# A state space front re-ordered: powers times coefficient first, its store moved to ScalarE, the first input products behind half a gate block

## The chip, the core and the metric

The kernel runs on one core of a Trainium2 chip. A core has a matrix engine (TensorE, PE in the profile), a vector engine (VectorE, DVE), a scalar engine (ScalarE, ACT), a general engine (GpSimd, POOL) and a synchronisation engine (SyncE, SP) that issues most of the transfers. Each engine runs its own list of instructions in the order in which it is written; semaphores tie the lists together. The metric is device microseconds (us) of one launch, median over several runs.

## The reference, cut to what matters

The network is a two-layer trunk over 1024 frames of 1024 channels. Layer 0 projects the normalised input to 6144 channels, which feed a state space branch (input u, gate), a retention branch (q, k, v, gate) and then one output projection; layer 1 is a convolution module. The change touches only the head of the state space branch. There each of 64 groups has 64 complex states, and from the step and the decay come the powers of the decay and a coefficient that scales the input matrix B:

```python
    lb_re = mag * jnp.cos(aim * dt)          # lambda-bar, one complex number per group and state
    lb_im = mag * jnp.sin(aim * dt)
    nr, ni = lb_re - 1.0, lb_im
    den = are * are + aim * aim
    coef_re = (nr * are + ni * aim) / den
    coef_im = (ni * are - nr * aim) / den
    bb_re = coef_re[..., None] * bre - coef_im[..., None] * bim
    bb_im = coef_re[..., None] * bim + coef_im[..., None] * bre
    ...
        bu_re = jnp.einsum('tbgh,gnh->tbgn', u_c, bb_re)
        bu_im = jnp.einsum('tbgh,gnh->tbgn', u_c, bb_im)
```

The states then run through a scan and are mapped back to channels by C, plus a skip term. All arithmetic is float32.

## The kernel before, in words

Everything is held transposed, channels on the 128 partitions, frames along the free side. A weight block is 128 output channels: it is loaded (`wf_`), split by ScalarE into a rounded high part (`wh_`) and by VectorE or GpSimd into a rest (`wl_`). A product of a block with one half of the frames (512) is 8 pieces of the inner dimension times three matmuls (lines 268 to 270: high times high, high times rest, rest times high), so a half block is 24 matmuls. The blocks come in a fixed sequence: `u0` to `u7` (the state space input), `g8` to `g23` (gates of both branches), then keys, queries, values and the later stages. Three banks of the accumulator (`ps_mm`) are used in turn by the halves, so a half can begin when the half three before it has been read out. A `u` half is read out by VectorE into `ut_` (line 464), a gate half into `gt_` (line 479).

Beside the `u` blocks VectorE works out the state space tables from the parameters (`s5_params`, lines 655 to 853): step, decay, sine and cosine, powers `s5_pr`, `s5_pi` (0 to 8), phases `s5_e1`, `s5_e2`, and the coefficient `s5_cfr`, `s5_cfi` (lines 820 to 839). Then two things use the coefficient: VectorE multiplies eight powers by it, six operations of 128x256 (line 842, helper line 676), giving `s5_pcr` and `s5_pci`; and GpSimd multiplies B by it, four products and two sums of 128x512 (lines 848 to 853), giving `s5_bbr` and `s5_bbi`.

`s5_turned` (line 871) turns `s5_pc` on TensorE (four 128x128 transposes into `turn`), ScalarE copies the bank to `turned` (line 882), and SyncE stores it to `pt_d` (line 883). ScalarE also copies `s5_bbr`, `s5_bbi` into block-diagonal form (`s5_bdr`, `s5_bdi`, line 887, two copies each).

The state space branch works in eight blocks B of 128 channels. For a block, `s5_tables` lets GpSimd make rotation tables `Tc`, `Ts` and the output table `W3` (lines 864 to 866, twelve operations), ScalarE make `R8` (line 939), and `s5_w2` load the turned powers from `pt_d`, spread over 16 partitions each (`PTr`, `PTi`, line 897), and B itself (`BTr`, `BTi`, line 901). ScalarE copies `PTr`, `PTi` to two banks (`pw0`, `pw1`, line 907), and six VectorE operations (lines 909 to 914) give the input matrices `W2r`, `W2i`. `s5_states` multiplies them with the input `U` (loaded by `s5_load`, line 944): eight matmuls of `v0` from `W2r` and eight of `v1` from `W2i` (line 962; the profile records each of these full float32 matmuls as two). The eight `kp` matmuls (lines 971, 973; 16 records) make the local kernel from `W3` and `s5_bd`; VectorE reads them as `Kg` (lines 976, 977), SyncE stores them to `k_d` in eight pieces and loads them back as `Wd` (lines 988, 992), and ScalarE copies that to `W1` (line 1027). VectorE turns and scans the states (lines 998 to 1005) and turns them back to `S` (lines 1012 to 1018). The `y` matmuls (lines 1044, 1048) use `S`, `W3`, `W1` and `U`.

The instructions are put in order by a scheduler that plays the program against a cost model and takes the oldest that is ready in that play; hand-written rules bind it: `ORDER` (lines 41 to 84) names an engine, a late instruction and an early one that has to come first, and `s5_order` (line 87) does so for VectorE in all eight blocks. `issue_after` adds such a rule for all instructions in its body.

Of the kernel before, what the change touches and what calls it, by code (L numbers as in the profile page):

```python
# [15 lines left out]
ALU = mybir.AluOpType  # L16
# [3 lines left out]
P = 128  # L20
# [20 lines left out]
ORDER = (  # L41
    ('PE', ('turn', 0), ('mm_u6_0', 23)),
    ('PE', ('mm_u6_1', 0), ('turn', 3)),
    ('PE', ('mm_g8_0', 0), ('v1_0', 7)),
    ('PE', ('kp_0', 0), ('mm_g8_0', 23)),
    ('PE', ('mm_g8_1', 0), ('kp_0', 7)),
    ('DVE', ('kraw_3', 0), ('yn_2', 0)),
    ('SP', ('gs1_3', 0), ('t_d', 7)),
    ('DVE', ('cv6_0', 23), ('h1l0_1', 0)),
# [89 lines left out]
class Trunk:  # L139
# [515 lines left out]
    def s5_params(self, sp, tp):  # L655
        nc, A = self.nc, self.A
        v = nc.vector
        n_ = [0]
        NP = 32

        def t(shape=(NP,), dt=F32, keep=None):
            n_[0] += 1
            if keep:
                return sp.tile([P, *shape], dt, name=keep)
            return tp.tile([P, *shape], dt, name=f"s5t{n_[0]}", tag=f"s5t_{'x'.join(map(str, shape))}_{dt}",
                           bufs=4 if shape[0] in (3, 4, 8) else 8)
# [8 lines left out]
        def tt(o, a, b, op, eng=v):  # L675
            return eng.tensor_tensor(o, a, b, op=op)
# [54 lines left out]
        r = t((2, NP))  # L731
# [86 lines left out]
        with self.tc.issue_after(self.last_phase.ins):  # L818
# [10 lines left out]
            cfr, cfi = t(keep="s5_cfr"), t(keep="s5_cfi")  # L829
# [10 lines left out]
        self.pc = [tp.tile([P, 8, NP], F32, name=f"s5_pc{c}") for c in "ri"]  # L840
        bc = lambda q: q[:].unsqueeze(1).broadcast_to([P, 8, NP])
        cmul(self.pc[0][:], self.pc[1][:], pr_[:, :8], pi_[:, :8], bc(cfr), bc(cfi), (8, NP))
        self.bb = [sp.tile([P, NP, 16], F32, name=f"s5_bb{c}") for c in "ri"]
        bc = lambda q: q[:].unsqueeze(2).broadcast_to([P, NP, 16])
        x2 = [tp.tile([P, 2, NP, 16], F32, name=f"s5bb{i}", tag="sq", bufs=2) for i in range(2)]
        x1 = [x2[i // 2][:, i % 2] for i in range(4)]
        gp = nc.gpsimd
# [23 lines left out]
    def s5_turned(self, pool):  # L871


        nc = self.nc
        self.pt_d = self.dram.tile([2, 2, P, P], F32, name="pt_d")
        ps = self.bank("turn")
        for c in range(2):
            for a in range(2):
                nc.tensor.transpose(ps[:, (2 * c + a) * P:(2 * c + a + 1) * P],
                                    self.pc[c][:, 4 * a:4 * a + 4, :].rearrange("p a b -> p (a b)"), self.ident[:])  # L880
        t = self.mid.tile([P, 4, P], F32, name="turned")
        nc.scalar.copy(t[:].rearrange("p q n -> p (q n)"), ps[:])
        nc.sync.dma_start(self.pt_d[:].rearrange("c a r n -> r (c a) n"), t[:])
        for q, t in zip(self.bd, self.bb):
            for g in range(2):
                r = slice(64 * g, 64 * g + 64)
                nc.scalar.copy(q[r, :, 16 * g:16 * g + 16], t[r])

    def s5_w2(self, B):

        nc, v = self.nc, self.nc.vector
        (ptr, pti), (btr, bti) = ([self.big(f"{n}{c}_{B}", f"{n}{c}", 1) for c in "ri"] for n in ("PT", "BT"))
        dp, db = self.pt_d, self.A["s5_bt"]

        with self.tc.issue_after(self.u_load.ins) if B else nullcontext():
            for c, pt in enumerate((ptr, pti)):
                nc.sync.dma_start(pt[:].rearrange("p q n -> p (q n)"),
                                  bass.AP(tensor=dp.tensor, offset=dp.offset + (c * 2 * P + 4 * B) * P,
                                          ap=[[32 * P, 8], [0, 16], [1, 4 * P]]))
            for c, bt in enumerate((btr, bti)):  # L900
                nc.sync.dma_start(bt[:].rearrange("p q n -> p (q n)"),
                                  bass.AP(tensor=db.tensor, offset=db.offset + (c * 4 * P + 4 * B) * P,
                                          ap=[[0, 8], [32 * P, 16], [1, 4 * P]]))
        w2r, w2i = (self.big(f"W2{nm}_{B}", f"W2{nm}", 1)[:].rearrange("p q n -> p (q n)") for nm in "ri")
        pr, pi = (self.ps_s5.tile([P, HALF], F32, name=f"pw{c}_{B}", tag=f"y{c}") for c in range(2))
        for bank, t in ((pr, ptr), (pi, pti)):
            nc.scalar.copy(bank[:], t[:].rearrange("p q n -> p (q n)"))  # L907
        br, bi = (t[:].rearrange("p q n -> p (q n)") for t in (btr, bti))
        v.tensor_tensor(w2r, pr[:], br, op=ALU.mult)
        v.tensor_tensor(w2i, pr[:], bi, op=ALU.mult)  # L910
        v.tensor_tensor(pr[:], pi[:], bi, op=ALU.mult)
        v.tensor_tensor(pi[:], pi[:], br, op=ALU.mult)
        v.tensor_tensor(w2r, w2r, pr[:], op=ALU.subtract)
        v.tensor_tensor(w2i, w2i, pi[:], op=ALU.add)
        return [t.rearrange("p (q n) -> p q n", q=4) for t in (w2r, w2i)]
# [25 lines left out]

    def s5_load(self, B):
        U = self.s5.tile([P, 8, P], F32, name=f"U_{B}", tag="U", bufs=2)
        self.u_load = self.nc.sync.dma_start(U[:], self.u_d[B].rearrange("j h g m -> (j h) g m"))
        return U

    def s5_states(self, B):
# [1100 lines left out]
```

## Time and profile before

| | us |
|---|---|
| median of 3 runs | 1133.97 (1131.9 to 1135.23) |
| the profiled execution's own time | 1132.57 |
| its span, first to last instruction | 1130.8 |
| TensorE busy in the span | 1116.0 |
| VectorE, GpSimd, ScalarE busy | 824.5, 592.8, 497.1 |
| mean granted TensorE clock | 0.994 of full speed |

The first column of a timeline row is the start in us from the span's start, the second the time to the end of the row's last instruction; then come engine, line, operation, output and inputs by the program's names without their numbers, and how many instructions the row merges. `[x <-E n Lm]` behind a row is idle time of the engine before it, and what ended it. SPq and ACTq are the sequencers of SyncE and ScalarE issuing a transfer: the row shows the issue, not the transfer. A matmul row's time overlaps that of the next; the pace is read from start to start. PEclk is the granted TensorE clock, 1.00 being full speed.

### The profile page before, as it was taken

What the parts mean: (1) busy time and instruction counts of PE and PEld (TensorE: products, weight loads), DVE (VectorE), ACT (ScalarE), POOL (GpSimd) and SP (SyncE); (2) the same over time, 40 slices, a digit from 0 to 9 for tenths busy, and PEclk for the clock granted to TensorE, in tenths of its full rate; (3) what the DMA queues carried; (4) which work ended last, traced back from release to release, by engine and by line L of the source; (5) the groups of instructions that cost most, each with busy time, mean ns of one, the idle gap of its engine ahead of it and who ended that gap; (6) DMA issues with size and microseconds to landing.
All of it is one profiled execution on the core that took longest, in us unless ns stands there. A gap on an engine that the chain in (4) does not pass through costs nothing.

```text
span 1130.8 us, 17173 instructions
## 1 busy us (share of the span) xinstructions
PE 1116.0 (99%) x6254; PEld 980.1 (87%) x6254; DVE 824.5 (73%) x1481; ACT 497.1 (44%) x729; POOL 592.8 (52%) x410
## 2 busy tenths in 40 slices
PE   9998999999999999999999999999999999999997
PEld 8877888888888888989888888888888888888886
DVE  7895777676516477696668532599999899999744
ACT  7322333333223231324346423545535677446773
POOL 3059766663126344333475110589544568778963
PEclk9998999999999999999999999999999999999999
DMA  8336455555468856958999998665778655356965
GB/s 321 114 104 203 141 170 192 172 183 166 144 234 284 305 185 191 320 192 309 384 387 311 330 332 282 196 230 202 239 257 290 243 193 177 124 173 222 331 256 179
DMA packets 125445, 261.99 MB, mean 232 GB/s; under 512 B 19760, under 2 KB 49328, under 8 KB 124720
## 3 DMA queue, kind: packets, MB, share of 16 engines
q1 hardware_dynamic: 121904, 248.30, 64.8%
q10 hardware_dynamic: 3456, 12.58, 2.8%
q8 instruction: 49, 0.80, 0.3%
q14 instruction: 36, 0.29, 0.1%
HBM read 182.53 MB, written 74.12 MB: 227 GB/s over the span
## 4 chain that ended last, share of the span: by engine, by line
PE 88%; DVE 5%; DMA 3%; ACT 1%; issue 1%; POOL 1%; SPq 0%; POOLq 0%; ACTq 0%; DVEq 0%
PE mm_g L268 7%; PE mm_g L269 7%; PE mm_g L270 7%; PE mm_wo L268 5%; PE mm_wo L270 5%; PE mm_wo L269 5%; PE mm_b L269 2%; PE mm_b L270 2%; PE mm_a L269 2%; PE mm_a L268 2%; PE mm_b L268 2%; PE mm_a L270 2%; PE mm_oc L269 2%; PE mm_oc L270 2%; PE mm_oc L268 2%; PE mm_glu L268 2%
## 5 line engine op out<-in xcount | busy, mean ns | idle before, releaser
L1660 DVE SCALAR_TENSOR_TENSOR cv<-u,convw,cv 128x512 f32<-128x512 f32 x390 | 268.0, 751 | 6.5 <-ACT cv L1627 4.4
L1621 POOL TENSOR_TENSOR tp<-tp,tp 128x512 f32<-128x512 f32 x64 | 82.5, 1289 | 33.4 <-ACT tp L1620 32.5
L268 PE MATMUL mm_g<-xh,wh_g 128*128 128x512 f32 x256 | 98.4, 384 | 0.0
L269 PE MATMUL mm_g<-xl,wh_g 128*128 128x512 f32 x256 | 97.4, 381 | 0.0
L270 PE MATMUL mm_g<-xh,wl_g 128*128 128x512 f32 x256 | 96.1, 380 | 0.0
L530 POOL TENSOR_TENSOR s1q<-s1q,s1q 128x512 f32<-128x512 f32 x12 | 17.2, 1432 | 80.6 <-ACT s1q L525 71.9
L1620 ACT ACTIVATE tp<-u,convw 128x512 f32<-128x512 f32 x64 | 45.3, 718 | 31.6 <-POOL tp L1621 30.9
L479 DVE TENSOR_TENSOR gt<-mm_g,R 128x512 f32<-128x512 f32 x32 | 22.0, 688 | 50.6 <-PE mm_g L270 50.6
L268 PEld LDWEIGHTS mm_g<-xh,wh_g 128*128 128x128 f32 x256 | 48.6, 190 | 7.2 <-ACT pw L907 0.3
L270 PEld LDWEIGHTS mm_g<-xh,wl_g 128*128 128x128 f32 x256 | 48.7, 190 | 7.0
L269 PEld LDWEIGHTS mm_g<-xl,wh_g 128*128 128x128 f32 x256 | 48.7, 190 | 6.7
L269 PE MATMUL mm_oc<-zl,wh_woc 128*128 128x512 f32 (+1 forms) x144 | 51.4, 357 | 0.2 <-DVE zl L1375 0.2
L268 PE MATMUL mm_oc<-zh,wh_woc 128*128 128x512 f32 (+1 forms) x144 | 51.1, 364 | 0.0
L270 PE MATMUL mm_oc<-zh,wl_woc 128*128 128x512 f32 (+1 forms) x144 | 50.8, 356 | 0.0
L268 PE MATMUL mm_wo<-ysh,wh_wos 128*128 128x512 f32 x128 | 48.9, 382 | 0.0
L268 PE MATMUL mm_g<-h1h,wh_cg 128*128 128x512 f32 x128 | 48.9, 382 | 0.0
L269 PE MATMUL mm_u<-xl,wh_u 128*128 128x512 f32 x128 | 48.8, 385 | 0.0
L270 PE MATMUL mm_b<-h1h,wl_cb 128*128 128x512 f32 x128 | 48.6, 379 | 0.0
L269 PE MATMUL mm_wo<-ysl,wh_wos 128*128 128x512 f32 x128 | 48.5, 379 | 0.0
L270 PE MATMUL mm_wo<-ysh,wl_wos 128*128 128x512 f32 x128 | 48.5, 379 | 0.0
L270 PE MATMUL mm_g<-h1h,wl_cg 128*128 128x512 f32 x128 | 48.5, 379 | 0.0
L268 PE MATMUL mm_a<-h1h,wh_ca 128*128 128x512 f32 x128 | 48.5, 379 | 0.0
(524 smaller groups left out, 3526.9 us busy)
## 6 DMA issues: line engine op xcount, KB each, us to landing
wf_g<-w_ab SPq DMA_DIRECT2D x16, 512.0 KB
wf_wos<-w_out SPq DMA_DIRECT2D x16, 512.0 KB
wf_wor<-w_out SPq DMA_DIRECT2D x16, 512.0 KB
wf_cb<-w_c SPq DMA_DIRECT2D x16, 512.0 KB
wf_ca<-w_c SPq DMA_DIRECT2D x16, 512.0 KB
wf_woc<-w_out_c SPq DMA_DIRECT2D x16, 512.0 KB
wf_v<-w_v SPq DMA_DIRECT2D x12, 512.0 KB
wf_cg<-w_c SPq DMA_DIRECT2D x11, 512.0 KB
```

The source lines that it names most:

```text
L268: nc.tensor.matmul(ps, wh[:, kb, :], xh, start=start, stop=False, **more)
L269: nc.tensor.matmul(ps, wh[:, kb, :], xl, start=False, stop=False, **more)
L270: self.last_mm = nc.tensor.matmul(ps, wl[:, kb, :], xh, start=False, stop=stop, **more)
L479: nc.vector.tensor_tensor(nat(gt[:, c]), un(ps[:]), nat(self.R[:, c]), op=ALU.mult)
L530: nc.gpsimd.tensor_tensor(a, a, sq[:], op=ALU.add)
L1620: nc.scalar.mul(sk[:], u[:, k:k + HALF], cw[:, nb, k:k + 1])
L1621: gp.tensor_tensor(s0[:], s0[:], sk[:], op=ALU.add)
L1660: v.scalar_tensor_tensor(dst[:], *tap, accs_[i][:], op0=ALU.mult, op1=ALU.add)
```

## The change

There are five pieces. (1) After the powers have been multiplied by the coefficient, VectorE makes a copy of the coefficient in one new tile `both`: two operations of 128x32 that also name `s5_pci` as an operand (with the operation `bypass`, which passes the first operand through), and GpSimd's six operations for B read that copy. They so begin only after `s5_pci` is written. (2) In `s5_turned` the store to `pt_d` is issued by ScalarE instead of SyncE, and the copies to `s5_bd` have to follow the copy to `turned`. (3) In `s5_w2` the loads for block 0 are written with B's before the powers', and for the other blocks the powers' before B's; (4) the load of `U` for block 1 has to follow the last of block 1's loads of powers and B. (5) `ORDER`: the first input products `v0`, `v1` of block 0 come after the first half of gate block `g8` instead of before it, the second half of `g8` comes after them, and VectorE reads out the first half of `u7` before the first of `W2r`.

```diff
 ORDER = (
     ('PE', ('turn', 0), ('mm_u6_0', 23)),
     ('PE', ('mm_u6_1', 0), ('turn', 3)),
-    ('PE', ('mm_g8_0', 0), ('v1_0', 7)),
+    ('PE', ('v0_0', 0), ('mm_g8_0', 23)),
+    ('PE', ('v1_0', 0), ('mm_g8_0', 23)),
     ('PE', ('kp_0', 0), ('mm_g8_0', 23)),
+    ('PE', ('mm_g8_1', 0), ('v1_0', 7)),
     ('PE', ('mm_g8_1', 0), ('kp_0', 7)),
+    ('DVE', ('W2r_0', 0), ('ut_7', 0)),
...
         cmul(self.pc[0][:], self.pc[1][:], pr_[:, :8], pi_[:, :8], bc(cfr), bc(cfi), (8, NP))
+        both, kept = t((2, NP)), self.pc[1]
+        tt(both[:, 0], cfr[:], kept[:, 0], ALU.bypass)
+        tt(both[:, 1], cfi[:], kept[:, 0], ALU.bypass)
+        cfr, cfi = both[:, 0], both[:, 1]
         self.bb = [sp.tile([P, NP, 16], F32, name=f"s5_bb{c}") for c in "ri"]
-        bc = lambda q: q[:].unsqueeze(2).broadcast_to([P, NP, 16])
+        bc = lambda q: q.unsqueeze(2).broadcast_to([P, NP, 16])
...
-        nc.scalar.copy(t[:].rearrange("p q n -> p (q n)"), ps[:])
-        nc.sync.dma_start(self.pt_d[:].rearrange("c a r n -> r (c a) n"), t[:])
+        copied = nc.scalar.copy(t[:].rearrange("p q n -> p (q n)"), ps[:])
+        nc.scalar.dma_start(self.pt_d[:].rearrange("c a r n -> r (c a) n"), t[:])
         for q, t in zip(self.bd, self.bb):
             for g in range(2):
                 r = slice(64 * g, 64 * g + 64)
-                nc.scalar.copy(q[r, :, 16 * g:16 * g + 16], t[r])
+                with self.tc.issue_after(copied.ins):
+                    nc.scalar.copy(q[r, :, 16 * g:16 * g + 16], t[r])
...
-            for c, pt in enumerate((ptr, pti)):
-                nc.sync.dma_start(pt[:].rearrange("p q n -> p (q n)"),
...
-            for c, bt in enumerate((btr, bti)):
-                nc.sync.dma_start(bt[:].rearrange("p q n -> p (q n)"),
...
+            loads = [[], []]
+            for c, (pt, bt) in enumerate(((ptr, btr), (pti, bti))):
+                loads[0].append((pt, bass.AP(tensor=dp.tensor, offset=dp.offset + (c * 2 * P + 4 * B) * P,
+                                             ap=[[32 * P, 8], [0, 16], [1, 4 * P]])))
+                loads[1].append((bt, bass.AP(tensor=db.tensor, offset=db.offset + (c * 4 * P + 4 * B) * P,
+                                             ap=[[0, 8], [32 * P, 16], [1, 4 * P]])))
+            for dst, src in chain(*(loads if B else loads[::-1])):
+                self.pt_load = nc.sync.dma_start(dst[:].rearrange("p q n -> p (q n)"), src)
...
         U = self.s5.tile([P, 8, P], F32, name=f"U_{B}", tag="U", bufs=2)
-        self.u_load = self.nc.sync.dma_start(U[:], self.u_d[B].rearrange("j h g m -> (j h) g m"))
+        with self.tc.issue_after(self.pt_load.ins) if B == 1 else nullcontext():
+            self.u_load = self.nc.sync.dma_start(U[:], self.u_d[B].rearrange("j h g m -> (j h) g m"))
```

What the scheduler makes of it shows at three places. The rows give line, operation, output, inputs and shape; the last number in a name is the buffer's, the one before it the block's (`pw0_1` is block 1's), and line numbers behind line 41 are higher in the changed kernel.

ScalarE around the copy of the turned powers, before:

```order
L257 CAST wh_g8_953<-wf_g8_952 128x1024
L887 COPY s5_bdr_485<-s5_bbr_742 64x32x16 x2
L887 COPY s5_bdi_486<-s5_bbi_743 64x32x16 x2
L882 COPY turned_878<-turn_873 128x512
L939 ACTIVATE R8_0_1094<-s5_s5_m01_491,s5_r8_621 128x128 x4
L257 CAST wh_g9_1013<-wf_g9_1012 128x1024
L907 COPY pw0_0_1109<-PTr_0_1099 128x512
```

and in the changed kernel:

```order
L260 CAST wh_g8_956<-wf_g8_955 128x1024
L889 COPY turned_881<-turn_876 128x512
L895 COPY s5_bdr_485<-s5_bbr_745 64x32x16 x2
L895 COPY s5_bdi_486<-s5_bbi_746 64x32x16 x2
L947 ACTIVATE R8_0_1097<-s5_s5_m01_491,s5_r8_621 128x128 x4
L890 DMA pt_d_875<-turned_881 128x4x128
L260 CAST wh_g9_1016<-wf_g9_1015 128x1024
L915 COPY pw0_0_1112<-PTr_0_1102 128x512
```

The copy `turned` has gone ahead of the four copies to `s5_bd`. The store of it, now on this engine, does not stand behind that copy but behind those four copies and the four operations of `R8`.

SyncE's transfers from the load of `U` for block 0 on, before:

```order
L944 DMA U_0_889<-u_d_84 128x1024
L901 DMA BTr_0_1101<-s5_bt 128x1x512
L883 DMA pt_d_872<-turned_878 128x4x128
L901 DMA BTi_0_1102<-s5_bt 128x1x512
L944 DMA U_1_1349<-u_d_84 128x1024
L897 DMA PTr_0_1099<-pt_d_872 128x1x512
L897 DMA PTi_0_1100<-pt_d_872 128x1x512
L472 DMA u_d_84<-ut_6_951 128x8x128
L255 DMA wf_g12_1443<-w_ab 128x1024
```

and in the changed kernel:

```order
L953 DMA U_0_892<-u_d_84 128x1024
L911 DMA BTr_0_1104<-s5_bt 128x1x512
L911 DMA BTi_0_1105<-s5_bt 128x1x512
L911 DMA PTr_0_1102<-pt_d_875 128x1x512
L911 DMA PTi_0_1103<-pt_d_875 128x1x512
L475 DMA u_d_84<-ut_6_954 128x8x128
L911 DMA PTr_1_1332<-pt_d_875 128x1x512
L258 DMA wf_g12_1446<-w_ab 128x1024
L911 DMA PTi_1_1333<-pt_d_875 128x1x512
L911 DMA BTi_1_1335<-s5_bt 128x1x512
L911 DMA BTr_1_1334<-s5_bt 128x1x512
L953 DMA U_1_1352<-u_d_84 128x1024
```

The store has left this queue, and the load of `U` for block 1, which stood ahead of block 0's loads of the powers, now stands behind all of block 1's loads.

TensorE at the end of the `u` blocks, before:

```order
L270 MATMUL mm_u7_1_1044<-xh_7_1_220,wl_u7_894 128x512
L962 MATMUL v0_0_1119<-U_0_889,W2r_0_1107 64x128 x8
L962 MATMUL v1_0_1128<-U_0_889,W2i_0_1108 64x128 x8
L268 MATMUL mm_g8_0_1188<-xh_0_0_140,wh_g8_953 128x512
L269 MATMUL mm_g8_0_1188<-xl_0_0_141,wh_g8_953 128x512
```

and in the changed kernel, where the first 23 rows of `mm_g8_0` stand ahead of these:

```order
L273 MATMUL mm_g8_0_1191<-xh_7_0_216,wl_g8_957 128x512
L971 MATMUL v0_0_1122<-U_0_892,W2r_0_1110 64x128 x8
L971 MATMUL v1_0_1131<-U_0_892,W2i_0_1111 64x128 x8
L980 MATMUL kp_0_1140<-W3_0_1080,s5_bdr_485 32x128 x4
L982 MATMUL kp_0_1140<-W3_0_1080,s5_bdi_486 32x128 x4
L271 MATMUL mm_g8_1_1218<-xh_0_1_144,wh_g8_956 128x512
```

The 24 matmuls of `mm_g8_0` have moved ahead of the 16 of `v0`, `v1`, and `kp` now follows `v1` directly. On VectorE the only other movement is the read-out of the first half of `u7`, from behind the six operations of `W2` to ahead of them.

More of the change, by code (lines that the diff above doesn't have):

```diff
@@ L895, in s5_w2 @@
         with self.tc.issue_after(self.u_load.ins) if B else nullcontext():
-            for c, pt in enumerate((ptr, pti)):
-                nc.sync.dma_start(pt[:].rearrange("p q n -> p (q n)"),
-                                  bass.AP(tensor=dp.tensor, offset=dp.offset + (c * 2 * P + 4 * B) * P,
-                                          ap=[[32 * P, 8], [0, 16], [1, 4 * P]]))
-            for c, bt in enumerate((btr, bti)):
-                nc.sync.dma_start(bt[:].rearrange("p q n -> p (q n)"),
-                                  bass.AP(tensor=db.tensor, offset=db.offset + (c * 4 * P + 4 * B) * P,
-                                          ap=[[0, 8], [32 * P, 16], [1, 4 * P]]))
+            loads = [[], []]
[6 more added lines that the diff above has]
+                self.pt_load = nc.sync.dma_start(dst[:].rearrange("p q n -> p (q n)"), src)
         w2r, w2i = (self.big(f"W2{nm}_{B}", f"W2{nm}", 1)[:].rearrange("p q n -> p (q n)") for nm in "ri")
```

## The prediction

> **What bounds the kernel now.** I read four views: the page, the list of whom TensorE waited for, the table of windows with the granted clock, and the chain of waits around the one long stall.
>
> From the page, the first row of part 1 and the clock in 40 slices:
>
> ```profile
> PE 1116.0 (99%) x6254; PEld 980.1 (87%) x6254; DVE 824.5 (73%) x1481; ACT 497.1 (44%) x729; POOL 592.8 (52%) x410
> PEclk9998999999999999999999999999999999999999
> ```
>
> TensorE is busy 99% of the span, so a gain exists only where it stands still or runs slowly. One slice, the fourth (85 to 113 us), shows a lower clock. All of TensorE's waits, longest first (us in total, times, longest):
>
> ```profile
> PE v L962 <- DVE W2r L913: 4.2, 1, 4.2
> ...
> PE turn L879 <- DVE s_pci L676: 1.0, 1, 1.0
> PE turn L879 <- DVE s_pcr L676: 0.8, 1, 0.8
> PE rf_ps L559 <- ACT s2q L1825: 0.6, 1, 0.6
> ```
>
> These three are what the change aims at; the row left out stands at the very start, and after them nothing longer than 0.6 us is left up to the end. What the waits cost is more than their length. Windows (us; busy time by engine; granted clock, DMA share, GB/s):
>
> ```profile
> 80.00:83.00 3.00, 3.00 (x9) 2.46 (x10) 3.00 (x3) 2.75 (x6) 3.00 (x2) 0.55 0.44 132
> 101.00:107.00 6.00, 5.17 (x36) 4.56 (x37) 4.77 (x8) 2.16 (x3) 5.84 (x6) 0.50 0.49 176
> ```
>
> After each stall the clock stands at half for a while. The TensorE timeline gives the whole loss:
>
> ```profile
> 77.33 0.38 PE L270 MATMUL mm_u<-xh,wl_u 128*128 128x512 f32 x1
> 79.92 0.44 PE L879 MATMUL turn<-ident,s_pci 128*128 128x128 f32 x2 [0.96 <-DVE s_pci L676]
> 80.12 0.63 PE L268 MATMUL mm_u<-xh,wh_u 128*128 128x512 f32 x1
> 87.72 0.38 PE L268 MATMUL mm_u<-xh,wh_u 128*128 128x512 f32 x1
> 97.21 0.38 PE L270 MATMUL mm_u<-xh,wl_u 128*128 128x512 f32 x1
> 111.56 0.38 PE L270 MATMUL mm_g<-xh,wl_g 128*128 128x512 f32 x1
> 155.34 1.09 PE L962 MATMUL v<-U,W2r 128*64 128x128 f32 x16
> 157.24 0.43 PE L971 MATMUL kp<-W,s_bdr 128*32 128x128 f32 x8
> ```
>
> From 87.72 to 97.21 lie 44 starts, 0.2157 us each: the full-speed pace; a half block of 24 takes 5.18. The half before the transposes ends its issue at 77.33 + 0.22 = 77.55. From there to the end of the last `u` half, 97.43, are four transposes (0.2 for two by the rows at 79.92 and 80.12, so 0.4) and three half blocks (15.53), 15.93 in all; it took 19.88. The first place costs **3.95 us**. From 97.43 to 111.78 (111.56 + 0.22) stand `v` and the half of `g8`: at full speed 1.90 (155.34 to 157.24, another block) and 5.18, together 7.08, and it took 14.35. The second costs **7.27 us**, 4.24 of it waiting and 3.0 half clock. So 11.2 us lie here, 1.0% of the run.
>
> Why `W2r` came late says the chain, in order of time:
>
> ```profile
> 73.28 4.90 POOL s5bb L676 x4
> 79.58 1.44 POOL s_bbi L676
> 83.98 6.84 DMA pt_d<-turned
> 90.89 0.61 SPq L897
> 91.55 7.70 DMA PTi<-pt_d
> 99.28 0.60 ACT pw L907
> 101.83 3.68 PE v L962 x32
> ```
>
> GpSimd's B held ScalarE, which held the store; then a store of 6.84 us and a load of 7.70 us followed each other, and 2.5 us of copy and products.
>
> **The change part by part.** *Powers first.* VectorE's operations of 128x256, alone and beside GpSimd's B:
>
> ```profile
> 64.03 0.42 DVE L676 TENSOR_TENSOR s5t<-s_e1i 128x256 f32<-128x256 f32 x1
> 64.36 0.42 DVE L676 TENSOR_TENSOR s5t<-s_e1r,s_e1i 128x256 f32<-128x256 f32 x1
> 73.24 0.42 DVE L676 TENSOR_TENSOR s5t<-s_pr,s_cfr 128x256 f32<-128x256 f32 x1
> 73.58 1.28 DVE L676 TENSOR_TENSOR s5t<-s_pi,s_cfi 128x256 f32<-128x256 f32 x1
> 79.79 1.10 DVE L464 TENSOR_TENSOR ut<-mm_u,R 128x512 f32<-128x512 f32 x1
> 80.80 1.29 DVE L258 TENSOR_TENSOR wl_g<-wf_g,wh_g 128x1024 fp32r<-128x1024 f32 x1
> ```
>
> Alone they start 0.33 apart, beside GpSimd each lasts 1.28. With GpSimd held back, six of them end at 73.24 + 6 x 0.335 = 75.25, before the last `u6_0` matmul at 77.33: both waits at the transposes go, with the half clock behind them. Gain 3.95 us, nothing chosen. The two small copies cost about 0.1 each on VectorE; the read-out behind them, held until 79.79 before, starts 4 us earlier. GpSimd's B starts at about 75.5 instead of 73.28. Its six rows lasted 7.7 us before; the `wl_g` row, which ran at 80.80 before, now falls among them and can hold one back by up to 1.3. So B ends between 83.2 and 84.5 (before: 81.0); I take 83.9.
>
> *The store.* The order shows it behind the four copies of B and `R8` on ScalarE, so it is not issued at once: the copies still wait for GpSimd. Rows of these, and of GpSimd's last operation for the table that `kp` needs:
>
> ```profile
> 81.04 1.25 ACT L887 COPY s_bdi<-s_bbi 64x512 f32<-64x512 f32 x2 [0.18 <-POOL s_bbi L676]
> 82.93 1.28 ACT L939 ACTIVATE R<-s_s_m,s_r 128x128 f32<-128x128 f32 x4
> 97.29 1.40 POOL L866 TENSOR_TENSOR W<-W,o 128x576 f32<-128x576 f32 x1
> ```
>
> The issue comes at 83.9 + 1.25 + 1.28 = 86.4, **2.4 us later** than before. Its transit should be shorter: the 512 KB loads ahead of it start some 4 us earlier, and `U` for block 1 no longer stands between it and the loads. Bounds: the quickest 512 KB transfer I find, and the slower 256 KB load of powers; above, 6.84 as before.
>
> ```profile
> 136.28 0.38 SPq L992 DMA_DIRECT2D Wd<-k_d  x1
> 139.72 1.05 ACT L1027 COPY W<-Wd 128x1024 f32<-128x1024 f32 x1 [0.44 <-DMA Wd<-k_d]
> 99.89 0.58 SPq L897 DMA_DIRECT2D PTi<-pt_d  x1
> 104.69 0.59 ACT L907 COPY pw<-PTi 128x512 f32<-128x512 f32 x1 [0.84 <-DMA PTi<-pt_d]
> ```
>
> That is 3.4 for the one (139.72 - 136.28) and 4.8 for the other. For the store I take 4.0, near the first, since it is a plain copy with only B's load in flight: landed at 90.4. The second load of powers is issued 0.66 later (91.55 against 90.89), 91.1; its transit lies between 4.8 and 7.7, and I take 6.0, nearer to the first because that transfer too had little ahead of it. `W2r` then needs 101.83 - 99.28 = 2.55: ready at 99.6. With both quick ends 97.8, with both slow ends 104.2.
>
> *The products behind half a gate block.* TensorE now reaches `v` at 77.55 + 15.93 + 5.18 = **98.7** without a wait: the half of `g8` needs only weights split before the transposes and a bank that VectorE reads out right behind `u6`. `v` so waits 99.6 - 98.7 = 0.9, between nothing and 5.5. `kp` behind it needs the row at 97.29 (done at 98.7), which moves with B's end by 2.9 to about 101.6; `kp`'s second half stands at 99.6 + 1.9 + 0.2 = 101.7, so it just fits, and each us that GpSimd is later costs one.
>
> *The rest.* For it, rows of ScalarE, VectorE and TensorE:
>
> ```profile
> 125.03 1.05 ACT L1027 COPY W<-Wd 128x1024 f32<-128x1024 f32 x1 [6.27 <-DMA Wd<-k_d]
> 97.74 0.69 DVE L909 TENSOR_TENSOR W2r<-pw,BTr 128x512 f32<-128x512 f32 x1 [7.87 <-ACT pw L907]
> 112.58 0.28 DVE L976 COPY Kg<-kp 128x112 f32<-128x112 f32 x1 [1.02 <-PE kp L973]
> 132.63 2.05 PE L1048 MATMUL y<-U,W 128*128 128x128 f32 x16
> ```
>
> VectorE's read-out of `u7`, moved ahead of `W2r`, falls into the 7.87 us in which VectorE waited for ScalarE's copy: nothing; without that cover it would push `W2r` back by its 1.1. The load of `U` for block 1 now goes out at about 99 and is used by block 1's `v` at about 118: nothing. SyncE's queue behind the powers' loads holds only `u` stores and weight loads for `g12`, used 30 us later. Behind `v`, the nearest deadline is `y` of block 0, the last of the rows: its input `W1` had 6.55 us to spare (126.08 to 132.63). TensorE comes there some 10 us earlier, its input only about 5 (VectorE read `kp` at 112.58, now right behind the scan, about 107.6). Some 1.3 us remain: nothing, but close.
>
> **Sum.** 3.95 + 7.27 - 0.9 = 10.3 us, if a wait of 0.9 does not halve the clock. The profiled execution had 1132.57 (span 1130.8); it becomes 1122.3. It lies 1.4 below the median of the runs, 1133.97, so by the median I forecast **1123.7**.
>
> The Trainium skill, TensorE: Matmul & The Clock Gate, section on the HAM clock gate, says that the clock falls to half only after a whole idle window of about 3.4 us. The windows above speak for a shorter one: the gap from 77.55 to 80.12, with transposes in it, was followed by 0.55. By that rule neither a wait of 0.9 nor one of 2.4 (first rival) would halve it, and the first rival's time would be 1125.2 by the median.
>
> **The rivals.** *Still late, still slow.* With the store at 5.2 and the load at 6.3 `v` waits 2.4 us, about as long as the gap at the transposes, and the clock halves: 11.2 - 2.4 - 3.0 = 5.8 gained, 1126.8, by the median 1128.2. For it: the second stretch of the chain took 7.70 with the store already done. Against: less is in flight.
>
> *The queue changes nothing.* Both transits stay as they were, 6.84 and 7.70: `W2r` at 104.2, 5.5 us of wait and 3.0 of half clock: 2.7 gained, 1129.9, by the median 1131.3, no measurable difference. Against it: before, the store stood right behind the loads of `U` and `BTr` in SyncE's queue. The Trainium skill, Trainium Kernel Development and Optimization, Key Constraints, supports this one: transfers issued from SyncE, ScalarE and GpSimd share the same 16 DMA engines, and issuing from several saves only issue time.
>
> *Absorbed at the next deadline.* `W1` for `y` of block 0 comes 2 us after TensorE wants it, with the half clock: 10.3 - 2 - 3 = 5.3 gained, by the median 1128.7. It decides if the load of `Wd` takes 3.3 us longer than before. Against: nothing new runs beside it.
>
> *Slower.* GpSimd's B ends so late that the store, now tied to it on ScalarE, drags everything. With the slow transits `v` starts 20.3 us after B's end (104.2 - 83.9). The gain is gone when `v` starts at 98.7 + 11.2 - 3.0 = 106.9, so from B's end at 86.6, and 0.3% is lost from 90.0. If the three read-outs (1.1 each) and the `wl_g` (1.29) that VectorE now runs beside B each held GpSimd back for their length, B would end at 83.2 + 4.6 = 87.8: 1.2 lost, by the median 1135.2. Against: before, GpSimd's four products took 4.90 beside VectorE's multiplications, little more than alone.
>
> That the store is issued right behind its copy is out: the order is fixed.
>
> **How the numbers follow.** Forecast 0.59, still late 0.20, the queue 0.08, absorbed 0.08, slower 0.05. A measurement of this kernel tells about 0.3%, 3.4 us, from no change. Faster: the forecast, the first rival and most of the absorbed one, 0.07, together 0.86; same: the queue, the rest of the absorbed one and 0.02 of the slower one, which at the price above stays inside 0.3%, 0.11; slower 0.03. Range: no wait at all gives 1121.4, by the median 1122.8, less 1.8 for spread, 1121.0; above, the first rival and the absorbed one with 1, 1129.5.
>
> **What would show it.** Right: no wait of TensorE at `turn`, `s_pci` written by 75.5, clock 1.00 through 80 to 84 us; the store issued at about 86.4 on ScalarE behind `R8`; one short wait or none at `v`, at about 99 us, and no clock below 0.9 after it; `y` of block 0 about 10 us earlier. Wrong: `v` beginning after 101, a wait at `kp` or at `y` of block 0, or B ending after 85.

## The result, and the profile after

The changed kernel takes **1122.92 us** (median of 4 runs, 1122.61 to 1123.15), the kernel before, timed beside it, 1133.59 (4 runs, 1131.9 to 1135.23). The ratio is 0.9906 with a 95% interval of 0.9889 to 0.9923: 10.7 us faster. The forecast was 1123.7, in a range of 1121.0 to 1129.5. The profiled execution took 1123.15, its span 1121.3 (before 1130.8).

From the page of the changed kernel, busy time and granted clock:

```profile
PE 1111.2 (99%) x6254; PEld 976.4 (87%) x6254; DVE 822.5 (73%) x1483; ACT 496.6 (44%) x729; POOL 593.5 (53%) x410
PEclk9999999999999999999999999999999999999999
```

The slice with the lowered clock is gone. TensorE's waits, and the two windows that were at 0.55 and 0.50:

```profile
PE idle L381 <- DVE mhalf L308: 1.1, 1, 1.1
PE ro L1344 <- DVE sc L1321: 0.7, 1, 0.7
```

```profile
80.00:83.00 3.00, 3.00 (x16) 2.62 (x15) 0.00 (x0) 0.61 (x1) 3.00 (x4) 1.00 0.90 306
101.00:107.00 6.00, 6.00 (x45) 5.09 (x42) 5.75 (x8) 1.56 (x2) 5.92 (x5) 1.00 0.71 236
```

Neither the transposes nor `v` stand in the list of waits. The row `ro`, much later in the program, was 0.2 before. The timeline of the changed kernel around the change, TensorE first, then VectorE, GpSimd, ScalarE and SyncE:

```profile
77.92 0.38 PE L886 MATMUL turn<-ident,s_pcr 128*128 128x128 f32 x2
98.86 0.38 PE L273 MATMUL mm_g<-xh,wl_g 128*128 128x512 f32 x1
99.17 1.09 PE L971 MATMUL v<-U,W2r 128*64 128x128 f32 x16
101.31 0.40 PE L982 MATMUL kp<-W,s_bdi 128*32 128x128 f32 x8
119.85 2.06 PE L1053 MATMUL y<-S,W 64*128 64x128 f32 x32
121.83 2.05 PE L1057 MATMUL y<-U,W 128*128 128x128 f32 x16
...
75.29 0.42 DVE L679 TENSOR_TENSOR s_pci<-s5t,s5t 128x256 f32<-128x256 f32 x1
75.95 1.09 DVE L467 TENSOR_TENSOR ut<-mm_u,R 128x512 f32<-128x512 f32 x1
76.96 1.21 DVE L261 TENSOR_TENSOR wl_g<-wf_g,wh_g 128x1024 fp32r<-128x1024 f32 x1
96.51 0.68 DVE L921 TENSOR_TENSOR W2r<-W2r,pw 128x512 f32<-128x512 f32 x1
...
82.32 1.27 POOL L679 TENSOR_TENSOR s_bbi<-s5bb 128x512 f32<-128x512 f32 x1
99.07 1.41 POOL L873 TENSOR_TENSOR W<-W,o 128x576 f32<-128x576 f32 x1
...
83.67 1.25 ACT L895 COPY s_bdi<-s_bbi 64x512 f32<-64x512 f32 x2
84.36 0.39 ACTq L890 DMA_DIRECT2D pt_d<-turned  x1
84.94 1.28 ACT L947 ACTIVATE R<-s_s_m,s_r 128x128 f32<-128x128 f32 x4
94.68 0.59 ACT L915 COPY pw<-PTi 128x512 f32<-128x512 f32 x1 [1.35 <-DMA PTi<-pt_d]
119.43 1.05 ACT L1036 COPY W<-Wd 128x1024 f32<-128x1024 f32 x1 [8.00 <-DMA Wd<-k_d]
...
77.07 0.36 SPq L475 DMA_DIRECT2D u_d<-ut  x1
78.60 0.45 SPq L953 DMA_DIRECT2D U<-u_d  x1
88.66 0.58 SPq L911 DMA_DIRECT2D PTr<-pt_d  x1
89.30 0.58 SPq L911 DMA_DIRECT2D PTi<-pt_d  x1
```

`W2r` is written at 97.2 (96.51 + 0.68) and TensorE comes to `v` at 99.08 (98.86 + 0.22), so `v` has 1.9 us to spare. From the end of the `u` half before the transposes to the first `y` row lie 119.85 - 77.92 = 41.93 us; before, they were 130.65 - 77.55 = 53.10. The 11.2 us that stood at the two places are all won there. The program reached the first place 0.4 us later than before (77.92 against 77.55), `y` therefore comes 10.8 us earlier (119.85 against 130.65), and the span is 9.5 shorter: 1.3 us are missing again behind `y`, of which the wait at `ro` shows 0.5. Neither can be put down to the change: in the fourteen traces of this study the first place is reached between 77.48 and 78.36 us, and the time from `y` to the end lies between 1000.1 and 1003.0.

### The profile page after: what moved, and what is told of

Same layout as the page of the kernel before. It is cut to its first block, busy times and chain, and to the rows that moved or that the text cites. A ratio compares the mean times of both kernels' runs of the same rounds, so it can differ in the third digit from the quotient of the medians.

```text
span 1121.3 us, 17174 instructions
## 1 busy us (share of the span) xinstructions
PE 1111.2 (99%) x6254; PEld 976.4 (87%) x6254; DVE 822.5 (73%) x1483; ACT 496.6 (44%) x729; POOL 593.5 (53%) x410
## 4 chain that ended last, share of the span: by engine, by line
PE 90%; DVE 3%; DMA 2%; ACT 2%; issue 1%; SPq 1%; POOL 0%; POOLq 0%; ACTq 0%; DVEq 0%
PE mm_g L271 7%; PE mm_g L272 7%; PE mm_g L273 7%; PE mm_wo L271 5%; PE mm_wo L273 5%; PE mm_wo L272 5%; PE mm_b L272 2%; PE mm_a L272 2%; PE mm_a L271 2%; PE mm_b L271 2%; PE mm_b L273 2%; PE mm_a L273 2%; PE mm_u L273 2%; PE mm_u L271 2%; PE mm_u L272 2%; PE mm_glu L271 2%
## 5 line engine op out<-in xcount | busy, mean ns | idle before, releaser
L272 PE MATMUL mm_a<-h1l,wh_ca 128*128 128x512 f32 x128 | 48.5, 379 | 0.0
```

The lines of the kernel that those rows point to most:

```text
L272: nc.tensor.matmul(ps, wh[:, kb, :], xl, start=False, stop=False, **more)
```

## The experiments

These 41.93 us turn out to be a floor: the four traces without a stall (the changed kernel, e4, e5, e6) agree on it to 0.01 us, so what a kernel loses between the transposes and `y` can be read off one trace. The table puts all runs on that measure; the sections behind it say what each was for. The median is that of all executions, the columns behind it are those of the one that was profiled. "From" is the end of the `u` half before the transposes (the start of its last row and 0.22), "to" the first `y` row, and "lost" what lies between them beyond 41.93.

| kernel | median us | from, to | lost | wait at transposes, at `v` | half clock for |
|---|---|---|---|---|---|
| before | 1133.59 | 77.55, 130.65 | 11.17 | 1.8, 4.2 | 3.4 and 6.8 |
| changed | 1122.92 | 77.92, 119.85 | 0 | 0, 0 | 0 |
| e1_powers_first | 1131.57 | 78.01, 129.01 | 9.07 | 0, 6.3 | 6.8 |
| e2_half_block_first | 1126.44 | 77.59, 121.72 | 2.20 | 1.8, 0 | 0 |
| e8_powers_and_order | 1123.99 | 78.14, 121.26 | 1.19 | 0, 1.1 | 0 |
| e9_without_powers_first | 1125.13 | 78.18, 124.00 | 3.89 | 1.8, 0 | 3.4 |
| e3_v_first | 1126.55 | 77.53, 124.48 | 5.02 | 0, 3.1 | 3.4 |
| e4_store_on_sync | 1123.25 | 77.56, 119.49 | 0 | 0, 0 | 0 |
| e5_loads_as_before | 1123.40 | 78.14, 120.07 | 0 | 0, 0 | 0 |
| e6_store_before_copies | 1122.55 | 77.48, 119.41 | 0 | 0, 0 | 0 |
| e7_store_early_v_first | 1127.07 | 78.19, 126.38 | 6.26 | 0, 3.2 | 6.8 |
| d6_w2r_later | 1125.43 | 77.71, 121.46 | 1.82 | 0, 1.7 | 0 |
| d9_w2r_later | 1129.19 | 77.81, 126.49 | 6.75 | 0, 4.0 | 6.8 |
| d12_w2r_later | 1131.63 | 78.36, 128.65 | 8.36 | 0, 6.1 | 6.8 |

The kernel before, timed beside the three sets, stood at 1133.26 (e1, e2, e3, e5), 1133.49 (e8 and the three d) and 1132.51 (e4, e6, e7, e9).

### One part alone: e1_powers_first, e2_half_block_first, and both: e8_powers_and_order

e1 is the kernel before with piece 1, e2 with piece 5, e8 with both; the store stays on SyncE and the loads in their old order.

```diff
 # e1, in s5_params
+        both, kept = t((2, NP)), self.pc[1]
+        tt(both[:, 0], cfr[:], kept[:, 0], ALU.bypass)
+        tt(both[:, 1], cfi[:], kept[:, 0], ALU.bypass)
+        cfr, cfi = both[:, 0], both[:, 1]
...
 # e2, in ORDER
-    ('PE', ('mm_g8_0', 0), ('v1_0', 7)),
+    ('PE', ('v0_0', 0), ('mm_g8_0', 23)),
+    ('PE', ('v1_0', 0), ('mm_g8_0', 23)),
...
+    ('PE', ('mm_g8_1', 0), ('v1_0', 7)),
+    ('DVE', ('W2r_0', 0), ('ut_7', 0)),
```

> The kernel before with the powers ahead of GpSimd's B and nothing else: `v` still stands ahead of the half of `g8`, and the store is still on SyncE behind the copies of B on ScalarE. My theory (the two gains hang together: time won at the transposes counts only if `v` does not wait for it): the waits at the transposes go and TensorE reaches `v` at 93.5 instead of 97.4, but B ends at about 83.6 instead of 81.0, so the store and with it W2r come 2.6 us later than before, at 104.4, unless the transfers are quicker; `v` waits about 11 us instead of 4.2, and the time is the time before or up to 2.9 us more, 1133.6 to 1136.5. Rival (the two places are independent, as my sum of 3.95 and 7.27 treats them): 3.95 us are won, 1129.6.

> The kernel before with the new order of TensorE and of the read-out of `u7` and nothing else: `v` behind the half of `g8`, the powers late as before. My theory: the waits at the transposes stay (1.8 us and the half clock, 3.95 in all), TensorE reaches `v` at 97.43 + 5.18 = 102.6, W2r is ready at 101.8, so `v` waits nothing and the clock stays at 1.00: 7.27 us are won, about 1126.3. Rival (the store's queue and the loads' order are what removes the wait): `v` still waits 2 us or more with half the clock after it, 1131 or more.

> The kernel before with powers first and `v` behind the half of `g8`, while the store stays on SyncE behind the copies of B and the loads stay in their old order. My theory (these two parts carry the gain, the store and the loads only give slack): with W2r at 100.4 as in e1_powers_first and TensorE at `v` at 99.3, `v` waits 1.1 us at most, without half clock: 1123 to 1124. Rival (the store and the loads carry a part of the gain of their own): the wait is 2 us or more, or the clock halves with it: 1126 or more.

Measured: e1 1131.57 (10 runs, ratio 0.9988, 0.9978 to 0.9999), e2 1126.44 (0.9934, 0.9919 to 0.9948), e8 1123.99 (0.9916, 0.9895 to 0.9937). So the half block alone wins 6.8 us, as expected, the powers alone 1.7, and both together 9.5. e8 came out as expected, in its time and in its wait of 1.1 at `v`. e1 lies between my range (1133.6 or more) and its rival (1129.6): alone, the powers are worth less than the 3.95 us that they were priced at. That the two gains fall short of the 9.5 when they are added up, by 1.0, is within the intervals and shows nothing. In e1, TensorE's longest wait, and rows of TensorE and SyncE:

```profile
PE v L966 <- DVE W2r L917: 6.3, 1, 6.3
```

```profile
78.01 0.38 PE L883 MATMUL turn<-ident,s_pcr 128*128 128x128 f32 x2
78.67 0.46 SPq L948 DMA_DIRECT2D U<-u_d  x1
85.61 0.38 SPq L887 DMA_DIRECT2D pt_d<-turned  x1
88.33 0.61 SPq L901 DMA_DIRECT2D PTr<-pt_d  x1
```

What the transposes no longer wait for, `v` waits for: 6.3 us instead of 4.2. I had expected 11, because I left the store at its 6.84 us; it took 2.7 (85.61 to 88.33). The likely reason is VectorE. In the kernel before, its read-out of a `u` half ends at 80.89 and the split of `g` at 82.09 (the quoted rows at 79.79 and 80.80), both behind the powers, and SyncE's `u` store, weight load and load of `U`, 512 KB each, go out behind them, right ahead of the store. The first and the last of these three, in the kernel before:

```profile
80.91 0.36 SPq L472 DMA_DIRECT2D u_d<-ut  x1
82.52 0.45 SPq L944 DMA_DIRECT2D U<-u_d  x1
```

With the powers first VectorE's two rows end at 77.0 and 78.2 (changed kernel), and the three transfers go out from 77.1 to 78.6. The cross of two kernels agrees: e9_without_powers_first has the store on ScalarE and no load of `U` for block 1 in front, but late powers, and its store took 6.1 us (its rows below); e1 has the old queue and order, but early powers, and took 2.7. The prediction had this as one of two reasons for a shorter store; it is the one that holds. e6_store_before_copies (below) bears it out: it has early powers, but its store goes out 0.6 us behind the load of `U` (78.73 and 78.17), and by the semaphore events of its trace it landed at 84.51, after 5.8 us, with the DMA engines' busy share at 1.03, 0.96 and 0.87 in the 2 us windows from 78 to 84. The three transfers do not explain why the store took 4.3 us in the changed kernel and 2.7 in e1. B's first load went out 0.7 us ahead of it in the one and 1.9 in the other (83.62 and 83.70), but no run separates this.

### The other parts left out: e9_without_powers_first, e3_v_first, e4_store_on_sync, e5_loads_as_before

Each is the changed kernel with one piece undone: e9 without the copy `both`; e3 with the old rule `('PE', ('mm_g8_0', 0), ('v1_0', 7))` in place of the new ones for TensorE; e5 with the old loop over the loads and without the rule on `U`; e4 as follows:

```diff
-        nc.scalar.dma_start(self.pt_d[:].rearrange("c a r n -> r (c a) n"), t[:])
+        nc.sync.dma_start(self.pt_d[:].rearrange("c a r n -> r (c a) n"), t[:])
```

> The changed kernel without the powers first: GpSimd's B starts beside VectorE's powers again, the other parts stay. My theory: the waits of 0.8 and 1.0 at the transposes return and the clock falls behind them in some executions (one stretch of 3.4 us, 1.7 lost) and not in others, as in e2_half_block_first; `v` does not wait: single times between 1124.7 and 1127.4. Rival (the 3.95 us of the prediction are lost each time): 1126.9.

> The changed kernel with `v` ahead of the half of `g8` again. My theory: TensorE reaches `v` at 93.9, W2r is ready at 97.2: a wait of 3.3 us, then half the clock over `v` and the half block for some 3 us more; about 6.3 us lost, 1129.2. Rival (the clock falls only after a longer idle time): 3.3 us lost, 1126.2, with a clock of 1.00 behind `v`. Rival (the quicker store and loads alone do it): no loss, 1122.9.

> The changed kernel with the store of the powers back on SyncE, between the two loads of B; its copy stays ahead of the copies of B on ScalarE. My theory (the queue is worth nothing: on ScalarE the store was held for GpSimd's B until 84.36, and on SyncE the load ahead of it is held for the same B until 83.62): store at about 84.5, W2r within 1 us of 97.2, no wait at `v`: 1122.9. Rival (the second queue is what shortened the store from 6.84 to 4.3 us): W2r at 99.7 or later, `v` waits 0.5 us or more: 1123.5 to 1126.

> The changed kernel with the loads in the order of the kernel before: the load of `U` for block 1 stands again between B's loads and the loads of powers. My theory: the store and the loads of powers share their time with 512 KB more and get slower by 1 to 2 us together, which the slack of 1.9 us at `v` nearly covers: 1122.9 to 1124. Rival (this order is what took the two transits from 6.84 and 7.70 to 4.3 and 5.4): W2r at about 102, `v` waits 2.8 us and the clock halves, about 1128.7.

Measured: e9 1125.13 (0.993, 0.9914 to 0.9947; single times 1123.71 to 1128.79), e3 1126.55 (0.9937, 0.9922 to 0.9952), e4 1123.25 (0.9922, 0.9903 to 0.994), e5 1123.40 (0.9905, 0.9887 to 0.9923). Without the powers first 2.2 us are lost, without the half block 3.6, without the new queue or the new order of loads nothing that can be told. e9's single times spread wider than the 1124.7 to 1127.4 that I expected, and its interval overlaps that of the changed kernel, so its 2.2 is rough. SyncE's queue in e4, and the same in e9 with the store, which is ScalarE's there, and the load of `U` for block 0:

```profile
84.17 0.38 SPq L890 DMA_DIRECT2D pt_d<-turned  x1
88.23 0.58 SPq L911 DMA_DIRECT2D PTr<-pt_d  x1
```

```profile
83.47 0.40 ACTq L886 DMA_DIRECT2D pt_d<-turned  x1
83.13 0.45 SPq L949 DMA_DIRECT2D U<-u_d  x1
89.55 0.58 SPq L907 DMA_DIRECT2D PTr<-pt_d  x1
```

On SyncE (e4) the store left at the same time as on ScalarE (84.17; the changed kernel 84.36) and landed after 4.1 us, against 4.3: the queue is worth nothing. The Trainium skill, DMA: Bandwidth & Descriptors, section "Issuing engines are not separate DMA queues", says that transfers started by ScalarE, SyncE or GpSimd run on the same 16 DMA engines; these two transits agree. The loads' order is worth 1.8 us of `W2r` (written at 99.2 in e5 after 97.2, with the program 0.2 later there) by my reading of the transits of the two loads of powers, 5.4 and 7.0 us instead of 4.1 and 5.4, but `v` begins at 99.4 there, so the slack of the changed kernel just covers it.

e3's `v` waited 3.1 us and I had put 3.0 of half clock on top; by the medians the whole loss was 3.6, in the profiled execution 5.0. Its windows are in the next part but one.

### The store still earlier: e6_store_before_copies, e7_store_early_v_first

```diff
-        nc.scalar.dma_start(self.pt_d[:].rearrange("c a r n -> r (c a) n"), t[:])
+        copied = nc.scalar.dma_start(self.pt_d[:].rearrange("c a r n -> r (c a) n"), t[:])
```

so that the copies of B follow the store, not only the copy `turned`. e7 has e3's rule as well.

> The changed kernel with the copies of B on ScalarE issued behind the store instead of ahead of it, so that only `turned`'s copy and `R8` stand before it. My theory: the store goes out at about 79.3, right behind the copy and while `R8` runs, since ScalarE's queue issues a transfer without waiting for the engine's work ahead of it where no data hangs on that; the loads of powers then follow B's loads at 85.1 and W2r is ready at about 93.7, 3.5 us earlier; the time stays 1122.9, since `v` did not wait. Rival (a transfer leaves in the engine's own order): the store at 80.5, behind `R8`. Rival (W2r still sets the time): faster than 1121.5.

> e6_store_before_copies with `v` ahead of the half of `g8` again, as in e3_v_first. My theory (the half block ahead of `v` buys time only because W2r is late): W2r at 93.7 meets TensorE, which comes at 93.7; a wait under 0.5 us, 1122.9 to 1123.5. Rival (the order is worth something of its own): `v` or `kp` waits 2 us or more, 1125.5 or more; here `kp` stands behind the half block as before, so only `v` is new.

Measured: e6 1122.55 (0.9913, 0.9898 to 0.9928), the changed kernel's time; e7 1127.07 (0.9958, 0.9939 to 0.9977), no better than e3. e6's ScalarE, SyncE and VectorE (the row at 85.39 is the second load of powers, the row at 93.76 what it released):

```profile
78.12 0.59 ACT L889 COPY turned<-turn 128x512 f32<-128x512 f32 x1 [4.78 <-PE turn L886]
78.60 0.40 ACT L947 ACTIVATE R<-s_s_m,s_r 128x128 f32<-128x128 f32 x1
78.73 0.39 ACTq L890 DMA_DIRECT2D pt_d<-turned  x1
78.90 0.97 ACT L947 ACTIVATE R<-s_s_m,s_r 128x128 f32<-128x128 f32 x3
93.76 0.59 ACT L915 COPY pw<-PTi 128x512 f32<-128x512 f32 x1 [0.78 <-DMA PTi<-pt_d]
85.39 0.58 SPq L911 DMA_DIRECT2D PTi<-pt_d  x1
95.67 0.68 DVE L921 TENSOR_TENSOR W2r<-W2r,pw 128x512 f32<-128x512 f32 x1
```

The store left at 78.73, 0.02 us after the copy and among the four operations of `R8` that stand ahead of it in the program: ScalarE's sequencer had passed them to the engine and gone on. But `W2r` came at 96.35, and not at 93.7. The second load of powers was issued 3.9 us earlier than in the changed kernel and landed only 0.9 earlier (the program stood 0.4 earlier there): it took 8.4 us, 85.39 to 93.76, in place of 5.4. Counted from each kernel's transposes, 5.2 us at the store gave 0.4 at `W2r`. So my expectation for e7 fell with it: with `W2r` as late as in e3, `v` waited the same 3.2 us. Why the loads, once issued right behind B's, took so long is open; the DMA engines' busy share was 0.30 to 0.71 in e6's windows of 2 us from 84 to 92, so on average they were not full.

### What a wait costs: d6_w2r_later, d9_w2r_later, d12_w2r_later

In the changed kernel, 6, 9 or 12 products more on VectorE ahead of the last for `W2r` of block 0 (each writes the first product of `W2i` once more); two rules keep `ut_7`'s second half and `kp` in their old places.

```diff
+        for _ in range(6 if B == 0 else 0):
+            v.tensor_tensor(w2i, pr[:], bi, op=ALU.mult)
         v.tensor_tensor(w2i, pr[:], bi, op=ALU.mult)
```

> The changed kernel with six more products of VectorE (the second product of W2 of block 0, written again with the same value) ahead of the last product for W2r, the order on TensorE unchanged. By the rows of 0.60 apart, less the 0.68 us that VectorE waited there for ScalarE's second copy, W2r comes 2.9 us later, at 100.1, and `v` waits about 0.95 us. Theory of windows (what the kernel before, e3_v_first and e1_powers_first show: the clock stands at half for one or two stretches of 3.4 us, and begins only where a stretch of that length was mostly idle): no half clock, only the wait, 1123.9. Theory of the prediction's first rival (any wait of 1 us or more halves it): 1126.9.

> As d6_w2r_later with nine more products: W2r 4.7 us later, at 101.9, and `v` waits about 2.75 us, as long as in the prediction's first rival. Theory of windows: the clock falls in some executions and not in others, as the wait lies to the stretches of 3.4 us; where it falls it costs 1.7 us on top: single times between 1125.7 and 1127.4. First rival of the prediction: always the wait and 3.0 us, 1128.7. Rule that only a whole idle stretch of 3.4 us halves the clock: always 1125.7, clock 1.00 throughout.

> As d6_w2r_later with twelve more products: W2r 6.5 us later, at 103.7, and `v` waits about 4.55 us, as in the kernel before. Theory of windows: in nearly every execution one or two stretches of 3.4 us at half clock, costing 1.7 to 2.5 us on top of the wait: 1129.2 to 1130. First rival of the prediction: the wait and 3.0: 1130.5. Without a price for the clock: 1127.5.

Measured: 1125.43 (single times 1124.14 to 1128.23), 1129.19 (7 runs, 1127.73 to 1130.52), 1131.63 (10 runs, 1129.83 to 1133.52). Each product took 0.72 us instead of 0.60, so the waits were 1.7, 4.0 and 6.1, longer than planned; the comparison has to be made with these. Windows whose bounds I set at the changes of the clock, of the kernel before (`v`), of e3, e9 (the transposes) and d9:

```profile
97.30:100.73 3.43, 0.29 (x2) 0.00 (x0) 2.12 (x4) 0.94 (x2) 3.43 (x3) 1.00 0.69 245
100.73:104.16 3.43, 2.33 (x22) 2.33 (x24) 3.43 (x5) 0.59 (x1) 3.35 (x4) 0.51 0.44 161
104.16:107.59 3.43, 3.43 (x19) 2.73 (x16) 2.20 (x5) 1.57 (x2) 3.35 (x3) 0.50 0.56 196
```

```profile
94.40:97.77 3.37, 0.98 (x18) 0.98 (x20) 2.92 (x5) 0.42 (x1) 3.29 (x4) 0.99 0.91 233
97.77:101.15 3.38, 3.38 (x23) 2.78 (x19) 1.99 (x4) 0.59 (x1) 3.30 (x3) 0.50 0.97 241
```

```profile
77.75:81.16 3.41, 1.65 (x9) 0.99 (x8) 3.41 (x4) 0.14 (x1) 3.41 (x3) 1.00 0.00 0
81.16:84.57 3.41, 3.41 (x10) 2.69 (x9) 2.60 (x4) 3.33 (x7) 3.41 (x3) 0.50 0.70 168
```

```profile
98.60:102.00 3.40, 0.54 (x3) 0.13 (x1) 3.19 (x6) 0.00 (x0) 3.32 (x4) 1.00 0.34 130
102.00:105.42 3.42, 2.26 (x22) 2.26 (x24) 2.72 (x4) 1.18 (x2) 3.34 (x3) 0.50 0.50 119
```

The third column is TensorE's busy time, the one before the last two the clock. The half clock lasts 3.4 or 6.8 us, in all eight places where it occurs between TensorE's first and last matmul in the traces of this study: it comes in whole stretches of 3.4 us. It follows a stretch in which TensorE was busy 0.29, 0.54, 0.98 or 1.65 us of 3.4, and ends behind a stretch that was busy throughout; one with 2.26 or 2.33 did not end it. The price is about half of TensorE's busy time in these stretches (in d9 2.26 and 3.42, so 2.8; lost beyond the wait were 2.7): from 1.7 to 3.1 us (e9 against e2 1.7; lost, less the wait: e3 1.9, d12 2.3, d9 2.7, e1 2.75, e7 3.1), and nothing where the wait does not empty a stretch (e8 with 1.1, d6 with 1.7).

Whether it does hangs on where the wait falls. At the transposes the same two waits of 0.8 and 1.0 were followed by half clock in the kernel before and in e9, and not in e2:

```profile
78.54 0.44 PE L882 MATMUL turn<-ident,s_pcr 128*128 128x128 f32 x2 [0.79 <-DVE s_pcr L679]
79.95 0.44 PE L882 MATMUL turn<-ident,s_pci 128*128 128x128 f32 x2 [0.97 <-DVE s_pci L679]
```

In each trace the changes of the clock lie whole multiples of 3.413 us apart. In the kernel before it falls at 80.29, at 100.77 and, behind the last matmul, at 1128.18 us, 6 and 307 multiples from the first. In e2 it falls only behind the last matmul, at 1120.42; counted back from there a stretch begins at 75.94 and the next at 79.35, so that the gap from 77.59 to 80.15 falls into both. In the kernel before and in e9 it lay within one (from 76.87 and from 77.75). These two of e2 and the one of d6 that holds its wait of 1.7:

```profile
75.94:79.35 3.41, 2.25 (x11) 1.45 (x9) 3.41 (x4) 0.00 (x0) 3.41 (x3) 1.00 0.00 0
79.35:82.76 3.41, 2.81 (x14) 2.52 (x15) 3.41 (x4) 2.89 (x5) 3.41 (x3) 1.00 0.29 88
```

```profile
99.35:102.76 3.41, 1.98 (x36) 1.81 (x40) 2.98 (x5) 1.18 (x2) 3.41 (x3) 1.00 0.53 147
```

On this grid no trace breaks the pattern: of the stretches at full clock every one with 1.65 us of work or less was followed by half clock, and none with 1.94 or more. Where the stretches lie against the program differs from trace to trace, so for a wait of this size the outcome of one execution is chance.

The loss at the transposes was 3.89 us with half clock (e9) and 2.20 without (e2). e3's four executions fit the same picture: those with a mean clock of 1.000 and 0.999 took 1126.19 and 1126.10, those with 0.997, of which one was profiled, took 1126.91 and 1127.35. (The fall behind the last matmul alone makes the mean 0.998 to 0.999 in the traces without a stall, so only the difference tells.) The Trainium skill, TensorE: Matmul & The Clock Gate, section on the HAM clock gate, says that the window of about 3.4 us runs freely and does not start anew with a kernel, which agrees with these traces; its condition for half clock, an idle window, is not what they show, since the clock fell behind stretches with up to 1.65 us of work.

The theory of windows so stands for the size and the place of the half clock. Its times for d9 and d12 were 1.8 and 1.6 us low, of which the longer waits explain 1.3 and 1.5. With waits as long as these a fixed 3.0 us on top of the wait would give nearly the same times, so d9 and d12 do not decide between the two; the traces of e8 and d6 do, where waits of 1.1 and 1.7 cost nothing on top. The prediction's own first rival, a wait of 2.4 us, no run has.

## Why the prediction was right, point by point

- **Powers first.** The last power was written at 75.71; the forecast was 75.25, and the program stood 0.4 later by then. Both waits went, the clock is 1.00 from 80 to 83. The 3.95 us are right for the execution that was read (e9: 3.89), but not each time: 2.20 in e2, where the clock stayed. The median without this piece was 2.2 higher.
- **B** ended at 83.59, inside 83.2 to 84.5.
- **The store** is the step that failed: "The issue comes at 83.9 + 1.25 + 1.28 = 86.4", because the order shows it behind `R8`. It came at 84.36, 0.8 us after GpSimd's B, while the last copy of B still ran (83.67 to 84.92) and before `R8` began (84.94). The order is that of the sequencer, which hands work to its engine and goes on; a place in the order is no time. The Trainium skill, Advanced Engine Details and Errata, section "Sequencer and Instruction Queues", describes this: engine instructions are pushed into a queue and further ones are read meanwhile. The copies of B ahead of it held it, as e6 shows; what the 0.8 us went on is not shown. e6 repeats it: with `R8`'s four operations ahead of it in the order the store left 0.02 us behind its copy, so the order does not keep a store from its copy either, as the prediction had it.
- **Transits.** Store 4.3 (forecast 4.0), second load of powers 5.4 (forecast 6.0). `W2r` was ready at 97.2 against 99.6: the issue came 2.0 us sooner and the load took 0.6 less, the store 0.3 more. `v` waited nothing against 0.9, so the forecast's sum was 0.9 us too careful in this term. Of the two reasons given for the shorter store the earlier 512 KB loads hold (e1, e9); the load of `U` for block 1 makes the loads of powers slower, not the store (e5: 4.4).
- **TensorE at `v`** at 99.08, forecast 98.7 without the 0.4 of the later start: exact.
- **The margins.** `W3` was done at 100.48 and `kp`'s second half began at 101.31: 0.8 us, more than the 0.1 forecast. `W1` was done at 120.48 for the `y` at 121.83: 1.35 us, forecast 1.3. No wait at either.
- **Sum.** Up to `y` 11.2 us were won, against 10.3. The profiled execution, forecast at 1122.3, still took 1123.15, because the 0.4 ahead of the change and the 1.3 behind `y` went the other way. The forecast then added 1.4 us, by which the execution that was read before lay below its median; that of the changed kernel lies 0.2 above its own. So errors of 0.9, 1.7 and 1.6 us nearly cancel, and that 1122.92 comes as near to 1123.7 as it does is in part luck.
- **The rivals.** "The queue changes nothing" had the right mechanism (e4) and the wrong consequence, since the transits changed for another reason. "Still late, still slow" needs 2.4 us of wait; with 1.7 (d6) no half clock shows in the trace, though one of its four executions had a mean clock of 0.995 and took 1128.23. "Absorbed at the next deadline" did not come, with 1.35 us left at `W1`, nor "slower": B ended at 83.59, 3 us ahead of the 86.6 where the gain would have gone.

## What to carry to other kernels

Where two stalls follow each other on one chain, price them together: time won at the first is only worth something if the work behind the second is ready by then (here the powers were priced at 3.95 us and won 1.7 alone, because the wait at `v` grew from 4.2 to 6.3). A cheap cure for a late operand is independent work put ahead of its consumer: a new order of 5.18 us of matmuls won 6.8 here, and where the operand came later still (e8, d6) only the rest was waited for. Read a store's lateness from what its sequencer must wait for, not from its place in the order or from the queue it is on, and look at what was issued shortly ahead of it: the store took 5.8 to 6.9 us where the nearest 512 KB transfer had gone out 0.3 to 1.5 us ahead of it, and 2.7 to 4.4 where that was 5.8 us or more.

## What the runs showed of the hardware that was not expected

- Half clock comes in whole stretches of 3.4 us (3.4 or 6.8 long, eight times of eight), on a grid that holds through an execution. It came behind a stretch with at most 1.65 us of work (1.94 or more did not bring it) and ended only behind one that was busy throughout; the same stall costs 2.2 or 3.9 us from one execution to the next.
- A transfer on ScalarE's queue is issued while earlier instructions of that engine still wait or run: at 78.73 among `R8`'s operations of 78.60 to 79.87.
- Loads of 256 KB issued 3.9 us earlier, right behind two others, landed only 0.9 us earlier (8.4 us in place of 5.4) at a DMA share of 0.3 to 0.71. What held them is open.
